# A half-shift of a matrix in memory: half rows cut per queue, or whole rows with wide reads

## The chip, the core and the metric

The kernel runs on one core of a Trainium2 chip. Its time is the device time of one execution in microseconds (us), given as the median of repeated runs. The kernel only moves data: the core has 16 DMA engines which copy from device memory (HBM) to device memory, and two of the core's instruction queues, SP's and ACT's, which hand them the work. No compute engine touches the data.

A word on terms. A DMA instruction names a source pattern and a destination pattern. The hardware turns each into descriptors, each one contiguous run of bytes. A packet, in the profile, is one recorded piece of work of one DMA engine.

## The reference

```
x: 8192 x 8192, float32
out = np.fft.ifftshift(x)
```

For even sizes this swaps the halves along both axes: `out[r, c] = x[(r + 4096) % 8192, (c + 4096) % 8192]`. Each output row is one input row with its left and right half (4096 elements, 16 KB each) exchanged. 268.44 MB are read and as many written. Nothing is computed.

## The kernel before, in words

In the code `R` and `C` are 8192, and `hr` and `hc`, 4096, are half of each. `ENGINES` and `per` are 16, so that one DMA covers `rows` = 256 rows of the output, but of each row only one half: 256 x 16 KB = 4 MB. The helper `copy` (line 29 issues the DMA) takes the queue, the first output row, and `h`, the column at which the written half begins: 0 for the left half, `hc` for the right one. The source half then begins at column `hc - h` of row `(row + hr) % R`.

Both sides of a DMA have the same pattern, in three dimensions: 16 steps of one row, then 16 steps of 16 rows, then 4096 elements side by side. The outermost dimension is the one that is dealt over the 16 DMA engines, so engine e copies rows e, e + 16, e + 32 and so on of the block. At a given moment the 16 engines are thus at work on neighbouring rows, 32 KB apart, and each engine goes on by 512 KB from one descriptor to the next. Every descriptor, read or write, is 16 KB.

The outer loop takes 1024 rows at a time, as four blocks. SP's queue writes the left halves of blocks 0, 1, 2, 3; ACT's queue writes the right halves of blocks 2, 3, 0, 1. The two halves of an output row are therefore written by different queues at different times, and likewise the two halves of an input row are read at different times. Each queue issues 32 DMAs.

The framework gives each DMA a completion semaphore out of four per queue. The first four DMAs of a queue go out at once; each later one waits for the DMA four places ahead of it in the same queue to land. Nothing else orders the work.

Of the kernel before, what the change touches and what calls it, by code (L numbers as in the profile page):

```python
# [1 line left out]

# [4 lines left out]


ENGINES = 16


@with_exitstack
def kernel(
    ctx: ExitStack,
    tc: tile.TileContext,
    x: bass.AP,
    out: bass.AP,
):
    nc = tc.nc
    R, C = x.shape  # L20
    hr = R // 2
    hc = C // 2
    per = 16
    rows = ENGINES * per

    def copy(queue, row, h, step):

        dims = [[C, ENGINES], [step * C, per], [1, hc]]
        queue.dma_start(
            out=bass.AP(out.tensor, out.offset + row * C + h, dims),  # L30
            in_=bass.AP(x.tensor, x.offset + (row + hr) % R * C + hc - h, dims),
        )

    for first in range(0, R, 4 * rows):
        for n in range(4):
            copy(nc.sync, first + n * rows, 0, ENGINES)
            copy(nc.scalar, first + (n + 2) % 4 * rows, hc, ENGINES)


# [1 line left out]
_INS = ['x']  # L43
_OUTS = [((8192, 8192), 'float32')]


def kernel(**inputs):
    import numpy as _np
    import concourse.bacc as _bacc
    import concourse.tile as _tile  # L50
    from concourse import mybir as _mybir
    from concourse.bass_utils import run_bass_kernel_spmd as _run

    nc = _bacc.Bacc("TRN2", target_bir_lowering=False, num_devices=1)  # L54
    arrays, args = {}, []
    for name in _INS:
        a = _np.ascontiguousarray(inputs[name])
        if a.dtype.kind in "iu":
            a = a.astype(_np.int64)
        arrays[f"in_{name}_dram"] = a  # L60
        args.append(nc.dram_tensor(f"in_{name}_dram", a.shape, _mybir.dt.from_np(a.dtype), kind="ExternalInput").ap())
    for i, (shape, dtype) in enumerate(_OUTS):
        dt = _mybir.dt.from_np(_np.dtype(dtype))
        args.append(nc.dram_tensor(f"out_{i}_dram", shape, dt, kind="ExternalOutput").ap())
    with _tile.TileContext(nc) as tc:
        kernel(tc, *args)
    r = _run(nc, [arrays], core_ids=[0])
    got = tuple(r.results[0][f"out_{i}_dram"] for i in range(len(_OUTS)))
    return got[0]
```

## Time and profile before

| what | value |
|---|---|
| time, median of 3 runs (lowest to highest) | 820.25 us (819.56 to 822.04) |
| profiled execution, span from its first to its last instruction | 812.4 us |
| profiled execution, its own device time | not recorded apart; the median lies 7.85 us above the span |
| DMA instructions | 32 on SP's queue, 32 on ACT's, 4 MB each |
| data packets | 16384 of 16 KB, half in each queue |
| mean rate of the copy, one direction | 330 GB/s over the span |
| compute engines | 0.2 us of POOL at the start |

The span begins with four small memory fills that every program of this framework makes. The row of digits for DMA in the page's view by slices is the busy share of the 16 DMA engines in tenths, and the row of GB/s is what they copied, in one direction; memory sees that rate twice, once as reads and once as writes. The view of queues counts the packets, those of a few bytes that raise semaphores among them. The view of DMA issues gives the time from the issue of a DMA to its landing. The view of waits for the DMA queues tells how long a queue stood before it could issue its next DMA, which costs nothing as long as the engines still have work.

### The profile page before, as it was taken

What the parts mean: (1) busy time and instruction counts of PE and PEld (TensorE: products, weight loads), DVE (VectorE), ACT (ScalarE), POOL (GpSimd) and SP (SyncE); (2) the same over time, 40 slices, a digit from 0 to 9 for tenths busy, and PEclk for the clock granted to TensorE, in tenths of its full rate; (3) what the DMA queues carried; (4) which work ended last, traced back from release to release, by engine and by line L of the source; (5) the groups of instructions that cost most, each with busy time, mean ns of one, the idle gap of its engine ahead of it and who ended that gap; (6) DMA issues with size and microseconds to landing.
All of it is one profiled execution on the core that took longest, in us unless ns stands there. A gap on an engine that the chain in (4) does not pass through costs nothing. (4 is left out here: it accounts for less than half of the span.)

```text
span 812.4 us, 109 instructions
## 1 busy us (share of the span) xinstructions
POOL 0.2 (0%) x4
## 2 busy tenths in 40 slices
POOL 0000000000000000000000000000000000000000
DMA  9999999999999999999999999999999999999998
GB/s 307 331 331 336 335 331 331 335 325 337 334 332 336 331 333 332 334 339 332 332 334 331 329 331 334 332 328 333 330 334 335 334 328 333 332 331 330 338 331 280
DMA packets 17408, 268.44 MB, mean 330 GB/s; under 512 B 1024, under 2 KB 1024, under 8 KB 1024
## 3 DMA queue, kind: packets, MB, share of 16 engines
q1 hardware_dynamic: 8704, 134.22, 49.7%
q10 hardware_dynamic: 8704, 134.22, 49.5%
HBM read 268.44 MB, written 268.44 MB: 661 GB/s over the span
## 5 line engine op out<-in xcount | busy, mean ns | idle before, releaser
L54 POOL MEMSET const-bfloat16-1.0<- 128x1 bf16 x1 | 0.1, 101 | 0.0
L54 POOL MEMSET const-uint8-127<- 128x1 uint8 x1 | 0.1, 101 | 0.0
L54 POOL MEMSET const-float32-0.0<- 128x1 f32 x1 | 0.1, 98 | 0.2 <-issue 0.2
L54 POOL MEMSET const-float32-1.0<- 128x1 f32 x1 | 0.1, 98 | 0.0
## 6 DMA issues: line engine op xcount, KB each, us to landing
out_dram<-in_x_dram SPq DMA_DIRECT2D x32, 4096.0 KB, 101.0
out_dram<-in_x_dram ACTq DMA_DIRECT2D x32, 4096.0 KB, 101.0
```

Of the source, the lines that this page charges most:

```text
L54: nc = _bacc.Bacc("TRN2", target_bir_lowering=False, num_devices=1)
```

## The change

Each DMA now takes 256 whole rows (8 MB) instead of 256 half rows (4 MB). The two patterns of a DMA no longer have the same shape. The source is 128 runs of two whole rows, 64 KB each. The destination is 256 rows of two half rows, 16 KB each, the right half first and then, by a negative step, the left one: read in order, the left half of an input row is what the right half of the output row wants. So 64 KB come in by one read descriptor and go out by four write descriptors. Because the ordinary call wants both sides to have the same shape, the DMA instruction is built directly.

The outermost dimension is now 128 long on the source and 256 long on the destination, and each of the 16 engines takes 8 of the one and 16 of the other. For both to mean the same rows, each engine's share must be 16 consecutive rows. At a given moment the 16 engines are thus at work on rows 16 apart, 512 KB, and each engine goes through 512 KB without a jump in the source.

SP's queue takes blocks 0, 2, 4 and so on, ACT's queue blocks 1, 3, 5 and so on. Each issues 16 DMAs, in the same scheme of four semaphores per queue: the first four go out at once and the later ones wait for the one four places ahead.

```
-    per = 16
-    rows = ENGINES * per
+    wide = 2
+    block = 256
-    def copy(queue, row, h, step):
+    def lowered(queue, tensor, offset, dims):
+        return queue.lower_ap_dma(bass.AP(tensor, offset, dims))
-        dims = [[C, ENGINES], [step * C, per], [1, hc]]
-        queue.dma_start(
-            out=bass.AP(out.tensor, out.offset + row * C + h, dims),
-            in_=bass.AP(x.tensor, x.offset + (row + hr) % R * C + hc - h, dims),
+    def copy(queue, name, row):
+        src = x.offset + (row + hr) % R * C
+        dst = out.offset + row * C + hc
+        queue.add_instruction(
+            mybir.InstDMACopy(
+                name=nc.get_next_instruction_name(),
+                queue=name,
+                mode="Copy",
+                ins=lowered(queue, x.tensor, src, [[wide * C, block // wide], [1, 1], [1, wide * C]]),
+                outs=lowered(queue, out.tensor, dst, [[C, block], [-hc, 2], [1, hc]]),
+            )
         )
-    for first in range(0, R, 4 * rows):
-        for n in range(4):
-            copy(nc.sync, first + n * rows, 0, ENGINES)
-            copy(nc.scalar, first + (n + 2) % 4 * rows, hc, ENGINES)
+    for first in range(0, R, 2 * block):
+        copy(nc.sync, "qSPDynamicHW", first)
+        copy(nc.scalar, "qActDynamicHW", first + block)
```

## The prediction

> **What bounds the kernel now.** I read the page's slices first, then its queues and issues, then the waits of the DMA queues, then short windows at both ends. The page by slices, queues and issues:
>
> ```profile
> span 812.4 us, 109 instructions
> ...
> DMA  9999999999999999999999999999999999999998
> GB/s 307 331 331 336 335 331 331 335 325 337 334 332 336 331 333 332 334 339 332 332 334 331 329 331 334 332 328 333 330 334 335 334 328 333 332 331 330 338 331 280
> DMA packets 17408, 268.44 MB, mean 330 GB/s; under 512 B 1024, under 2 KB 1024, under 8 KB 1024
> ...
> q1 hardware_dynamic: 8704, 134.22, 49.7%
> q10 hardware_dynamic: 8704, 134.22, 49.5%
> HBM read 268.44 MB, written 268.44 MB: 661 GB/s over the span
> ...
> out_dram<-in_x_dram SPq DMA_DIRECT2D x32, 4096.0 KB, 101.0
> out_dram<-in_x_dram ACTq DMA_DIRECT2D x32, 4096.0 KB, 101.0
> ```
>
> The engines hold packets for 99.2% of the span (49.7 + 49.5), so no idle time between DMAs is left to win. The rate is flat: apart from the first and the last slice of 20.3 us it lies between 325 and 339 GB/s. The 17408 packets are 16384 of data and 1024 of a few bytes for semaphores. One data packet takes on average 0.992 x 812.4 us x 16 / 16384 = 787 ns. Among the packet records of this trace the shortest full packets, and a quarter of all of them, take about 611 ns; many take over 1000. An engine can thus pass 16 KB in 611 ns, or 429 GB/s over 16 engines, and mostly does not: on average 176 ns of a packet, 22%, are waiting within it. Since neither queue nor engine is idle, I put this waiting down to memory, which serves 661 GB/s of reads and writes together. Which part of memory it is, this trace doesn't show.
>
> The waits of the DMA queues, with their total, number and longest in us:
>
> ```profile
> SPq L29 <- DMA out_dram<-in_x_dram: 689.4, 28, 25.3
> SPq L65 <- DMA out_dram<-in_x_dram: 102.2, 2, 79.5
> ```
>
> SP's queue waits 28 times, about 25 us each, but a DMA lands 101 us after its issue. Four are always under way, so these waits starve no engine. Short windows at both ends (start and end, us, POOL, clock, DMA share, GB/s):
>
> ```profile
> 0.00:2.00 2.00, 0.20 (x4) 1.00 0.00 0
> 2.00:4.00 2.00, 0.00 (x0) 1.00 1.03 336
> ...
> 806.00:808.00 2.00, 0.00 (x0) 1.00 0.96 328
> 808.00:810.00 2.00, 0.00 (x0) 1.00 0.54 180
> 810.00:812.40 2.40, 0.00 (x0) 1.00 0.02 7
> ```
>
> The data moves from 2.0 us to about 809.5, that is 807.5 us at 332.4 GB/s, with some 5 us of edges. The sum is made against this execution: span 812.4, and the median of the runs, 820.25, is 7.85 more; I carry these 7.85 over unchanged.
>
> **The change part by part.**
>
> *Fewer descriptors.* Reads go from 16384 to 4096; writes stay at 16384. What a descriptor costs by itself is bounded by the small packets: the 4-byte semaphore packets take 9 ns, and an 8 KB record of 307 ns against the 611 leaves 611 - 2 x 307, below zero, so nothing. An engine handles 768 read descriptors fewer (12288 / 16): 0 to 768 x 9 ns = 6.9 us. I take 0, since a cost of 9 ns lies under the 176 ns that the mean packet waits for memory anyway; if memory stopped being the limit, up to 6.9 us would come free.
>
> *Half as many DMAs.* 32 instead of 64, so per engine 32 semaphore packets fewer: 32 x 9 ns = 0.3 us off. The issue itself (571 ns on SP's queue, 578 on ACT's) happens beside running transfers, except the first, which keeps its place: data still starts at about 2.0 us. There are 12 waits for a DMA four ahead on each queue instead of 28. With 8 MB per DMA each queue gets half of 332.4 GB/s and lands one in about 50 us, some 200 us after issue. Behind each wait stands only the next DMA of the same queue, with three more under way: 0.
>
> *The end.* All engines carry 16.8 MB as before, and now end in the records within about 2.4 us of each other. If an engine turns from one queue to the other only after a 64 KB read, that unit takes 4 x 787 ns = 3.1 us instead of 0.8, and the last engine can be late by up to the difference. Bounds 0 and +2.4 us; I take +1, between them, because the present spread is already about three small units.
>
> *The order in which memory is touched.* This is the term that decides. Before, each engine reads and writes 16 KB and jumps 512 KB; the two halves of a row are used at different times. After, each engine runs through 512 KB of source in order, and the destination in order but for the swap within each 32 KB row. On the other hand the engines stand 512 KB apart instead of 32 KB, in step at the start of every DMA. No row of the trace prices either. The bounds: at best the wait within packets disappears, 1024 packets x 611 ns = 626 us of transfer instead of 807.5, -181 us. At worst the rate is that of the poorest short slice; the DMA view of the last 112 us, in slices of 2.8 us, shows them:
>
> ```profile
> GB/s 304 357 363 281 357 328 351 345 310 334 316 328 334 357 298 351 304 369 316 293 427 281 363 310 351 304 363 363 298 339 310 357 334 322 304 351 357 304 310 29
> ```
>
> Apart from the end the poorest is 281: 268.44 MB / 281 GB/s = 955 us, +148. Both ends are extremes of a moment that the average never held. The rows nearest to a steady pattern are the 20 us slices: 339 GB/s at best and 325 at worst, i.e. 792 us (-15.6) or 826 us (+18.5). [...]
>
> As a limit on the gain, the Trainium skill (HBM Reference, Specifications) gives a memory domain about 716 GB/s. The trace's 661 agrees in being below it; 536.9 MB at 716 would be an estimated 750 us of transfer, and the sum with it about 763 us, so by that page a large part of the 181 us is out of reach.
>
> **The sum.** 820.25 - 15.6 (order) + 1.0 (end) - 0.3 (semaphores) + 0 (descriptors, waits) = 805.4 us. I say 805.
>
> **The rivals.**
>
> *Streams collide (slower).* The sixteen engines stand at a distance of a power of two, 512 KB, twice (for reads and for writes). If they ask the same part of memory at once, the waiting within packets grows. Place: the 176 ns per packet. Price: at the poorest 20 us slice, 325 GB/s, 820.25 + 18.5 + 0.7 = 839; half way from there to the poorest short slice, 303 GB/s, 886 us transfer and 899. It decides as soon as the mean packet is over 787 ns, whatever the reads gain. For it: packet times scatter from 611 to over 1000 ns, so memory already reacts to which addresses meet; the old order kept the engines on neighbouring rows. Against it: the scatter soon takes engines out of step, within one DMA of 32 units each. Chance 0.37.
>
> The Trainium skill speaks for this rival (DMA: Bandwidth & Descriptors, Latency and other measured facts): copies with rows a large power of two apart lose rate, 207 GB/s at a pitch of 512 KiB against 214 in full, and 164 at 2 MiB. Taken over to the distance between engines, that ratio is an estimated 807.5 x 214/207 = 835 us of transfer and 848 us in all; no run here shows it yet.
>
> *Nothing moves.* Memory serves 661 GB/s whatever the order, and only the end and the semaphores differ: 820.25 + 1 - 0.3 = 821. For it: the flat slices, 325 to 339 all along, while SP and ACT meet different addresses. Against it: nobody has shown that the 22% of waiting is indifferent to order. Chance 0.09.
>
> *Only the descriptors pay.* The read side has a fixed cost which is on the path after all: 820.25 - 3.5 (half of the 6.9) + 0.7 = 817. Chance 0.07.
>
> *The read is taken whole before it is written,* or the wide read is not spread over 16 engines. If a 64 KB read and its four writes no longer overlapped, a 64 KB unit would take up to twice 4 x 611 ns; 256 units x 4.9 us = 1251 us. Against it: 128 and 256 both divide by 16, and in the present trace reads and writes share one packet of 611 ns. Chance 0.06.
>
> *The change doesn't do what it says.* The hardware may cut the 64 KB reads into 16 KB. Then the order in memory still changes, and the forecast or the first rival holds; only the 3.1 us unit falls away. No chance of its own.
>
> **How the numbers follow.** The forecast's case, a better rate, has 0.41; its own range is 789 to 817, from twice the step of the best slice down to a quarter of it. A measurement of this kernel tells 0.3%, or 2.5 us, from no change, which is the band 817.8 to 822.7. Faster: 0.41 + 0.07 = 0.48. Same: 0.09. Slower: 0.37 + 0.06 = 0.43. The range must take in much of the slower cases: from 782 (two and a half such steps; 0.04 below) to 880, which leaves out the 0.06 of unoverlapped reads and about 0.09 of heavy collisions.
>
> **What would show it.** DMA packets: 4096 of 64 KB if the wide read is the unit, 16384 if the writes are. DMA share still about 99%, mean rate 339, issues x16 with 8192 KB landing in about 200 us. A collision shows as the same share with under 330 GB/s; a lost overlap as a rate under 250; uneven engines as a long last slice. What would make me wrong is above all the one term of memory order, chosen between +148 and -181 by the nearest slices.

## The result and the profile after

The changed kernel takes 867.58 us (median of 4 runs, 867.10 to 868.31) against 821.10 us for the kernel before measured beside it (median of 4, 819.56 to 822.04): a ratio of 1.0567, 95% interval 1.0544 to 1.0590. It is slower by 5.7%. The forecast was 805, so the sign is wrong, though the range reached to 880. Of the times and ratios below, one leaves a run out: the kernel with shares of 15 rows took 832.29 to 836.07 us in three runs and 868.30 in a fourth, which is not counted.

The page of the changed kernel, with the lines that answer to those shown before:

```profile
span 865.4 us, 77 instructions
...
DMA  9999999999999999999999999999999999999998
GB/s 285 311 310 311 309 314 314 314 312 305 307 315 313 313 304 311 310 314 317 305 317 313 314 314 311 310 315 314 312 314 304 313 314 316 307 310 314 316 309 276
DMA packets 16896, 268.44 MB, mean 310 GB/s; under 512 B 512, under 2 KB 512, under 8 KB 512
...
q10 hardware_dynamic: 8448, 134.22, 49.9%
q1 hardware_dynamic: 8448, 134.22, 49.5%
HBM read 268.44 MB, written 268.44 MB: 620 GB/s over the span
...
out_dram<-in_x_dram ACTq DMA_DIRECT2D x16, 8192.0 KB, 215.0
out_dram<-in_x_dram SPq DMA_DIRECT2D x16, 8192.0 KB, 215.2
```

Three things are to be seen. First, the loss is spread evenly: the engines hold packets for 99.4% of the span, as before, but the rate is 304 to 317 GB/s in the inner slices instead of 325 to 339. A data packet takes 0.994 x 865.4 us x 16 / 16384 = 840 ns on average instead of 787; 16384 / 16 = 1024 packets per engine times those 53 ns are 54 us, and the span grew by 53.0. Nothing is lost between packets or at the ends. Second, of the 16896 packets 512 raise semaphores and 16384 carry data, 16 KB each. There is no packet of 64 KB. Third, a DMA lands 215 us after its issue, where some 200 were foreseen.

The 53.0 us between the spans are more than the 46.5 by which the times differ, because the two profiles do not match: in every run that has both, the time is 1.7 to 2.2 us above the span, so the profiled execution of the kernel before took an estimated 814 us, less than any of its four timed runs. The 7.85 us that the prediction carried over were mostly this difference between executions.

The short windows of the changed kernel (start and end, us, POOL, clock, DMA share, GB/s) show the same start and a short end:

```profile
2.00:4.00 2.00, 0.00 (x0) 1.00 0.98 262
...
200.00:400.00 200.00, 0.00 (x0) 1.00 1.00 311
400.00:600.00 200.00, 0.00 (x0) 1.00 1.00 313
...
860.00:862.00 2.00, 0.00 (x0) 1.00 1.00 295
862.00:865.40 3.40, 0.00 (x0) 1.00 0.33 106
```

The source line of the issue has one surprise, in ns, as least, median and greatest; the kernel before comes first:

```profile
L29 SPq DMA_DIRECT2D out_dram<-in_x_dram x32: 571/571/652, 0.7 to 708.6; - x32
...
L36 SPq DMA_DIRECT2D out_dram<-in_x_dram x16: 554/43836/50956, 0.7 to 647.1; - x16
```

An issue took 0.57 us before and now typically 43.8: the queue is held for that long before it can go on. That looks like a cause, and the experiments test it.

What the compiler made of the change can be read from the DMA instruction itself, as pairs of step (in elements) and count:

```
before         source  [8192, 16] [131072, 16] [1, 4096]
               dest    [8192, 16] [131072, 16] [1, 4096]
changed kernel source  [4096, 512] [1, 1] [1, 4096]
               dest    [8192, 256] [-4096, 2] [1, 4096]
```

The source asked for 128 runs of two rows. Lowering it against a destination with pieces of 4096 elements cut it into 512 pieces of 16 KB, one behind the other. So the wide reads of 64 KB, of which the change was to be made, are not in the instruction; the encoded length of a source piece is 16384 bytes. What is left of the change is the order of addresses, the larger DMA, and a source and a destination whose patterns are no longer alike: one dimension of 512 here, 256 by 2 there. Two descriptions of equal length and equal piece, but of unlike shape.

### The profile page after: what moved, and what is told of

The parts are those of the page before. It is cut to its first block, busy times and chain, and to the rows that moved or that the text cites. A ratio compares the mean times of both kernels' runs of the same rounds, so it can differ in the third digit from the quotient of the medians.

```text
span 865.4 us, 77 instructions
## 1 busy us (share of the span) xinstructions
POOL 0.2 (0%) x4
## 2 busy tenths in 40 slices
DMA packets 16896, 268.44 MB, mean 310 GB/s; under 512 B 512, under 2 KB 512, under 8 KB 512
```

## The experiments

All times are medians; every ratio is to the kernel before measured beside it, with its 95% interval. There the kernel before took 812 to 814 us.

**First: which part of the change costs it?** Theory 1 was the distance of 512 KB between the engines, the rival of the prediction.

Engines 512 KB apart, half rows as before:

```
-        dims = [[C, ENGINES], [step * C, per], [1, hc]]
+        dims = [[step * C, ENGINES], [C, per], [1, hc]]
```

> The kernel before with one edit: engine e takes rows 16e to 16e+15 of the block instead of e, e+16, e+32. The engines are then 512 KB apart, as in the changed kernel; half rows, 4 MB DMAs and the pairing of the queues stay. Theory 1 (the distance of 512 KB between the engines costs the time): 855 to 875 us, rate near 310 GB/s. Rival A (the reads, DMA size or the two halves in one DMA cost it): 815 to 826 us.

Measured: 812.26 us, 1.0004 (0.9978 to 1.0030). The distance alone costs nothing.

The source written as 16 KB reads:

```
-ins=lowered(..., src, [[wide * C, block // wide], [1, 1], [1, wide * C]])
+ins=lowered(..., src, [[C, block], [hc, 2], [1, hc]])
```

> The changed kernel with the source pattern written as two half rows of 16 KB per row, in the same order of addresses. Since the compiled instruction of the changed kernel already holds 512 reads of 16 KB, all theories that I still hold expect 865 to 870 us. The theory that wide reads cost the time expects 815 to 830 us.

Measured: 848.39 us, 1.0449 (1.0412 to 1.0485). It compiles to the same DMA instructions as the changed kernel, so this is also a second measurement of that: 4.5% here, 5.7% in the first comparison, where the kernel before was slower too (821.1 against 812.3). Its span of 846.9 us gives 822 ns for a data packet, so 35 of the 53 ns above come back, and 36 of the 46.5 us. Why the same instructions cost more in the first comparison is not explained.

Shares of 15 rows instead of 16:

```
-    block = 256
+    share = 15      # blocks of 240 rows; the last 16 rows of each half as one small DMA
```

> The changed kernel in blocks of 240 rows (a rest of 16 rows in each half of the matrix goes as one small DMA): engines are 15 rows, 480 KB, apart instead of 16 rows, 512 KB. Theory 1a (what costs is that the distance is a power of two): 800 to 830 us. Theory 1b (what costs is that engines are far apart at all): 860 to 875 us. Rival A (DMA size or the halves in one DMA): 860 to 875 us.

Measured: 834.15 us, 1.0289 (1.0234 to 1.0344), between the two expectations. With theory 1 gone this told little by itself; it finds its place below.

DMAs of 8 MB, rows dealt as before:

```
-    per = 16
+    per = 32
-            copy(nc.scalar, first + (n + 2) % 4 * rows, hc, ENGINES)
+            copy(nc.scalar, first + (n ^ 1) * rows, hc, ENGINES)
```

> The kernel before with 512 rows in a DMA instead of 256, that is 8 MB as in the changed kernel, with the queues still 16 MB apart; rows are dealt to the engines as before. Theory 1: 817 to 824 us, though the queues now block in the issue for some 44 us per DMA. Rival B (DMAs too large for the queue, whose issue blocks): 850 to 875 us.

Measured: 813.45 us, 1.0009 (0.9977 to 1.0041), with an issue of 41.1 us at the median on SP's queue. So the long issue by itself costs nothing.

**Second: the queues' distance, or neighbouring halves?** Theory 2 blamed the 8 MB between the queues; theory 3 the step from one half of a row straight to the other.

```
 queues 8 MB apart (kernel before):
-            copy(nc.scalar, first + (n + 2) % 4 * rows, hc, ENGINES)
+            copy(nc.scalar, first + (n ^ 1) * rows, hc, ENGINES)
```

> The kernel before with the queues 256 rows (8 MB) apart instead of 512 rows (16 MB); nothing else. Theory 2 (the two queues at 8 MB, not 16 MB, collide): about 4.5 per cent over the kernel before, 845 to 860 us. Theory 3 (what costs is that one queue of an engine takes both halves of a row one right after the other): within 0.5 per cent of before.

Measured: 812.15 us, 0.9995 (0.9970 to 1.0020).

```
 queues 16 MB apart (changed kernel):
-        copy(nc.scalar, "qActDynamicHW", first + block)
+        for row in (first, first + block):      # first in steps of 4 * block
+            copy(nc.sync, "qSPDynamicHW", row)
+            copy(nc.scalar, "qActDynamicHW", row + 2 * block)
```

> The changed kernel with the queues 512 rows (16 MB) apart instead of 256 rows. Theory 2: within 1 per cent of the kernel before. Theory 3: 4 to 6 per cent over it, as the changed kernel.

Measured: 850.16 us, 1.0454 (1.0418 to 1.0491). Theory 2 falls with these two.

```
 the other half first (changed kernel):
-        ins ... [[wide * C, block // wide], [1, 1], [1, wide * C]]   outs ... [[C, block], [-hc, 2], [1, hc]]
+        ins ... [[C, block], [-hc, 2], [1, hc]]                      outs ... [[C, block], [hc, 2], [1, hc]]
```

> The changed kernel with the two halves of each row taken in the other order: the source goes right half, left half, and the destination is written in order. Theory 3, and theory 2 too: 4 to 6 per cent over the kernel before. If only the backward step of the writes were at fault, within 1 per cent of the kernel before.

Measured: 848.05 us, 1.0413 (1.0398 to 1.0429). Writing backwards is not the fault. Note that now the destination is the single run of 512 pieces and the source is 256 by 2.

```
 halves in two DMAs (kernel before, shares of 16 rows):
+        for h in (hc, 0):
+            copy(nc.sync, first, h, ENGINES)
+            copy(nc.scalar, first + rows, h, ENGINES)
```

> Whole rows in the changed kernel's order of blocks and with its engine shares (16 consecutive rows) and queues 8 MB apart, but each block as two half-row DMAs of 4 MB one behind the other, first the right halves, then the left ones. Theory 2: 4 to 6 per cent over the kernel before. Theory 3: within 1 per cent of it, since a queue now meets the second half of a row only 16 descriptors per engine later.

Measured: 813.08 us, 0.9985 (0.9969 to 1.0002). Theory 3 stood here, four expectations out of four.

**Third: what about the neighbouring halves?**

```
 left half of one block, right half of the next, by turns:
-        ins ... [[wide * C, block // wide], [1, 1], [1, wide * C]]   outs ... [[C, block], [-hc, 2], [1, hc]]
+        ins ... [[C, block], [other * C + hc, 2], [1, hc]]           outs ... [[C, block], [other * C - hc, 2], [1, hc]]
```

> Still half rows of 16 KB, 8 MB DMAs and shares of 16 rows, and still left and right halves by turns in one DMA as in the changed kernel, but the right half belongs to the row 256 rows further on (on ACT's queue, further back). No two descriptors in a row touch neighbouring memory any more. Theory 3 (the cost is that an engine's queue goes from one half of a row straight to the other, 16 KB away): within 1 per cent of the kernel before. Rival C (the pattern of a DMA with two halves by turns costs it, wherever they lie): 4 to 6 per cent over it.

Measured: 815.17 us, 1.0012 (0.9990 to 1.0034), as theory 3 expects; but this run is not clean, since the framework took the writes of the two queues for overlapping and let ACT's DMAs wait for SP's. It shows by accident what the long issue hangs on. The two queues issue DMAs of the same size, but ACT's has only one or two under way, as one lands after 61.7 us and the next goes out about 50 us after the last:

```profile
L35 SPq DMA_DIRECT2D out_dram<-in_x_dram x16: 573/40488/48138, 0.7 to 582.5; - x16
L35 ACTq DMA_DIRECT2D out_dram<-in_x_dram x16: 580/582/648, 28.5 to 784.9; - x16
```

In the changed kernel, too, the first three issues of each queue take under 1 us, and the fourth is the first to be held. The hold goes with what already waits in the queue, not with the size of one DMA alone.

```
 no exchange of columns, right half before left on both sides:
-        ins ... [[wide * C, block // wide], [1, 1], [1, wide * C]]
+        ins ... [[C, block], [-hc, 2], [1, hc]]      # src begins at + hc
```

> The changed kernel without the exchange of left and right (the columns stay, so that part of the computation is left out): both sides go right half, left half, row by row. Neighbouring halves follow each other, but neither side is one unbroken run that hardware could join to longer pieces. Theory 3a (neighbouring halves in a row cost it by themselves): 4 to 6 per cent over the kernel before. Theory 3b (it costs only where one side is an unbroken run and the other not): within 1 per cent.

Measured: 813.30 us, 0.9995 (0.9976 to 1.0013). Neighbouring halves are free: theory 3 falls as first put, and 3b or something about the exchange is left.

```
 one row per engine and DMA:
-    block = 256
+    block = 16
```

> The changed kernel in blocks of 16 rows, so that an engine takes one row of a DMA (two descriptors) and the engines are one row, 32 KB, apart as in the kernel before; 512 DMAs of 512 KB. Theory 3 alone: 4 to 6 per cent over the kernel before. If the neighbouring halves cost only together with a great distance of the engines (as the 2.9 per cent at 15 rows suggests): within 1 per cent of it. Issue: 256 DMAs per queue, each about 0.6 us, against 3.2 us that a queue has for one, so nothing from there.

Measured: 819.29 us, 1.0068 (1.0048 to 1.0088), within the second expectation.

```
 64 KB on both sides, no exchange:
-        outs ... [[C, block], [-hc, 2], [1, hc]]
+        outs ... [[wide * C, block // wide], [1, 1], [1, wide * C]]
```

> Whole rows without the exchange of left and right (that part of the computation is left out), with 64 KB descriptors on both sides, engines 512 KB apart, 8 MB DMAs: what wide descriptors are worth where both sides can have them. Theory 3a: 4 to 6 per cent over the kernel before, since an engine runs through neighbouring memory. My prediction's view (long runs help memory): 1 to 4 per cent under it.

Measured: 813.82 us, 0.9995 (0.9978 to 1.0011). Its page shows that wide descriptors would have been visible as packets:

```profile
DMA packets 4608, 268.44 MB, mean 331 GB/s; under 512 B 512, under 2 KB 512, under 8 KB 512
...
HBM read 268.44 MB, written 268.44 MB: 661 GB/s over the span
```

4608 less 512 for semaphores are 4096 packets of 64 KB. They run at the rate of the kernel before, neither better nor worse: the view that long runs help memory is refuted here, where long runs really exist.

**Fourth: do reads and writes meet in memory?** Theory 4 held that an engine reads one half while it writes the same half 4096 rows away.

```
 kernel before, both queues on the same rows:
-            copy(nc.scalar, first + (n + 2) % 4 * rows, hc, ENGINES)
+            copy(nc.scalar, first + n * rows, hc, ENGINES)
```

> The kernel before with ACT's queue on the same rows as SP's instead of 512 rows away, so that an engine alternates between the two halves of the same rows, one queue reading the half that the other is writing the counterpart of. Theory 4 (reads and writes collide when one engine reads column half h of an input row while it writes column half h of the output row exactly 4096 rows from it, so at an unchanging distance of 128 MB in the two tensors): 2 to 6 per cent over the kernel before. Rival D (the cost needs both halves as consecutive descriptors of one DMA): within 0.7 per cent.

Measured: 813.30 us, 0.9990 (0.9963 to 1.0017).

```
 changed kernel, source 256 rows further on:
-        src = x.offset + (row + hr) % R * C
+        src = x.offset + (row + hr + block) % R * C
```

> The changed kernel with the source 256 rows (8 MB) further on, so that the rows are shifted by 4352 instead of 4096 (that part of the computation is altered); order, halves and shares stay. Theory 4: within 1 per cent of the kernel before, since the halves read and written together no longer stand exactly 128 MB apart. Rival D (neighbouring halves taken in exchange cost it, wherever the rows are written to): 4 to 6 per cent over it.

Measured: 847.99 us, 1.0431 (1.0399 to 1.0464). Against theory 4 on both counts.

```
 changed kernel, four rows per engine and DMA:
-    block = 256
+    block = 64
```

> The changed kernel in blocks of 64 rows: the engines are 4 rows, 128 KB, apart, queues 2 MB apart, 2 MB a DMA. With 32 KB between the engines the loss was 0.7 per cent, with 512 KB 4 to 5.7. If the loss grows with the distance of the engines: 1 to 4 per cent over the kernel before. If it needs the great distance: under 1 per cent.

Measured: 811.84 us, 0.9980 (0.9958 to 1.0003). This was the strangest so far: the changed kernel's order, halves and exchange, in 2 MB pieces, at the speed of the kernel before.

```
 as the queues on the same rows, with shares of 16 rows:
+        dims = [[step * C, ENGINES], [C, per], [1, hc]]
+            copy(nc.scalar, first + n * rows, hc, ENGINES)
```

> The kernel before with both edits at once: ACT's queue on the same rows as SP's, and shares of 16 consecutive rows, so that the engines are 512 KB apart. Theory 4, with the distance making it worse: 4 to 6 per cent over the kernel before and more than with the rows dealt out. Rival D: within 0.7 per cent.

Measured: 813.53 us, 1.0003 (0.9981 to 1.0025). Theory 4 is dead.

**Fifth: order of addresses, or unlike patterns?** All slow kernels up to here have the unlike patterns described above, and every DMA in them that matters is large. Two kernels take the pair apart. The trick is to begin the second half of a source row 256 bytes early: the two halves then no longer join to one run, and the source keeps its shape of 256 by 2.

```
 like patterns, the changed kernel's order with the exchange:
-        ins ... [[wide * C, block // wide], [1, 1], [1, wide * C]]
+        ins ... [[C, block], [hc - 64, 2], [1, hc]]
 compiled: source [8192, 256] [4032, 2] [1, 4096]   dest [8192, 256] [-4096, 2] [1, 4096]
```

> The changed kernel, but the second half of each source row begins 64 elements (256 bytes) earlier, so that source and destination keep the same shape of 256 rows by 2 halves, where the compiled source of the changed kernel is one run of 512 pieces of 16 KB. The addresses are otherwise the same (64 columns of each left half come out altered). Theory 5 (the order of addresses costs it: neighbouring halves, exchanged, with engines 512 KB apart): 4 to 6 per cent over the kernel before. Theory 6 (the unlike patterns of the two sides cost it, in DMAs of some size): within 1 per cent of the kernel before.

```
 unlike patterns, a plain copy without the exchange:
+        ins ... [[C, block], [hc - 64, 2], [1, hc]]
+        outs ... [[C, block], [hc, 2], [1, hc]]       # dst begins at row * C
 compiled: source [8192, 256] [4032, 2] [1, 4096]   dest [4096, 512] [1, 1] [1, 4096]
```

> Whole rows without the exchange of left and right (left out; 64 columns of each right half come out altered too), with the source in 256 rows by 2 halves, the second 256 bytes early, and the destination as one run of 512 pieces of 16 KB. Theory 5: within 1 per cent of the kernel before, like the kernels without the exchange. Theory 6: 3 to 6 per cent over it, with the addresses of a plain copy.

Measured: like patterns 813.61 us, 1.0016 (0.9996 to 1.0037); unlike patterns 847.01 us, 1.0438 (1.0390 to 1.0485). The pages, like patterns first:

```profile
span 810.8 us, 77 instructions
...
DMA packets 16896, 268.44 MB, mean 331 GB/s; under 512 B 512, under 2 KB 512, under 8 KB 512
...
HBM read 268.44 MB, written 268.44 MB: 662 GB/s over the span
```

and the unlike ones:

```profile
span 844.1 us, 77 instructions
...
DMA packets 16896, 268.44 MB, mean 318 GB/s; under 512 B 512, under 2 KB 512, under 8 KB 512
...
HBM read 268.44 MB, written 268.44 MB: 636 GB/s over the span
```

The same packets, the same number of DMAs of the same size, the same early 256 bytes. The changed kernel's addresses without its unlike patterns are as fast as the kernel before; a plain copy with unlike patterns is as slow as the changed kernel. Theory 6 holds so far: it is the description of the two sides, not where the data lies.

One thing is not taken apart. In every slow kernel one side is a single dimension of 512 pieces (480 with shares of 15 rows) and the other side is not. No run has 512 pieces of 16 KB in one dimension on both sides, or two unlike sides of which neither is such a run. That the unlikeness costs the time, and not the one long dimension by itself, is therefore argued, not shown; 64 KB on both sides has one dimension on each and is fast, but with 8 pieces per engine it is also small in pieces.

A view of the issues of the like kernel, in ns, closes the other suspicion:

```profile
L35 SPq DMA_DIRECT2D out_dram<-in_x_dram x16: 573/41074/46916, 0.7 to 607.0; - x16
```

It is held for 41 us per issue just as the slow one is for 44, and loses nothing by it.

The size belongs to it. With unlike patterns, by pieces of 16 KB that one engine gets from one DMA:

| pieces per engine and DMA | rows in a block | ratio to the kernel before |
|---|---|---|
| 2 | 16 | 1.0068 |
| 8 | 64 | 0.9980 |
| 30 | 240 | 1.0289 |
| 32 | 256 | 1.0413 to 1.0567 |

The 0.7% of the first line may be its 512 DMAs; no run separates that. Where between 8 and 30 the loss begins was not tried.

The large ones are also those whose issue is held: in the kernel with 64 rows SP's median issue is 553 ns. It would fit that the loss comes from handing out the descriptors, or from a full queue. The end of the traces speaks against both, as far as they would have to act while the data moves. In the kernel with unlike patterns the last issue is over at 677.5 us, and from 793.5 us on only the last DMA of each queue is under way; in the one with like patterns this is so from 650.6 and 762.8 us on. The rates before and after the second moment, unlike patterns first:

```profile
680.00:790.00 110.00, 0.00 (x0) 1.00 1.00 319
794.00:838.00 44.00, 0.00 (x0) 1.00 0.99 320
```

```profile
652.00:760.00 108.00, 0.00 (x0) 1.00 1.00 332
764.00:805.00 41.00, 0.00 (x0) 1.00 0.99 334
```

The loss of 4% stays when nothing is being issued, and when an engine has at most 32 pieces left from each queue. The kernel with 64 rows has as many under way, four DMAs of 8 pieces, and loses nothing. So, as far as these traces reach, the loss goes with the size of the single DMA and not with how much is under way. What happens inside such a DMA stays open: no trace here separates a packet's wait for its descriptor from its wait for memory.

## Why the prediction was wrong

The sum failed at two terms. The order of addresses was put at -15.6 us and is worth nothing. And the sum had no term for what the change did to the patterns of a DMA, which is the whole loss: with the order at 0 it gives 821 us, and the 46.6 us from there to 867.6 are missing, or 34 to 36 by the later comparisons. That 867.6 still lies in the stated range is luck, since the range went up to 880 for collisions, which no run shows.

*The change doesn't do what it says.* This was the rival to which I gave no chance of its own, and it is what happened: the reads were cut to 16 KB, as the 16384 data packets and the compiled pattern show, though by the lowering and not by the hardware. I wrote that then only the order in memory remains. That was the blind spot: the two patterns had also become unlike, one of them a single long dimension, and this is where the time went. The patterns after lowering could have been read before the run; I read only the source text.

*The order in which memory is touched,* taken at -15.6 us, is the step of the sum that failed. No run shows a gain from it. With like patterns the changed kernel's order measures +0.16% (-0.04 to +0.37), or about +1 us, and real 64 KB runs -0.05% (-0.22 to +0.11). The right value was 0. Picking the best 20 us slice as a price was not a bound on anything: the slices of one kernel scatter by themselves, and say nothing of another pattern.

*Streams collide* came close in its time (839, or 899 for the heavier case, against 867.6) and lay on the right side, but not by its mechanism: engines 512 KB apart cost 1.0004. The rule that I set beside it, the Trainium skill (DMA: Bandwidth & Descriptors, Latency and other measured facts), has rows 512 KiB apart at 207 GB/s against 214. Carried over to the distance between engines it would have given some 3%; the runs measure 0.0% (-0.2 to +0.3), so it doesn't carry over to this pattern. That the estimate from it, 848 us, is what the same instructions took in the later comparisons (847 to 850) is chance.

*Fewer descriptors* at 0: right, though the reads did not become fewer. Where they truly do, with 64 KB on both sides, nothing is gained either, so the 0 to 6.9 us that was kept as a bound is closed at its lower end.

*Half as many DMAs,* waits at 0: right. The 8 MB DMAs alone measure 1.0009. The landing was put at 200 us; it is 202 with like patterns and 215 in the changed kernel. But I had the issue at 0.57 us, and it is 44. It stayed hidden, as the 8 MB DMAs alone show; I take it that this is because several DMAs are always under way.

*The end,* +1 us: there is no 64 KB unit, so its reason is gone. The last window holds 106 GB/s over 3.4 us, 0.36 MB, or 1.2 us at the usual rate.

*The limit on the rate.* The waiting within packets that I put down to memory is 176 ns in the kernel before. Of what the change added to a packet, 53 ns in the first comparison and 35 in the second, none that the runs can tell is due to the order of addresses in memory, as the like and unlike kernels show. Whether the 176 ns are, is still open: the kernels with like patterns all stand at 658 to 665 GB/s whatever their order, which fits a common ceiling and does not name it.

## What to carry to other kernels

When a DMA is written with a different pattern on each side, read what the compiler made of both before reasoning about descriptor sizes: a contiguous side may be folded into one long dimension and cut to the piece size of the other. Keep the two sides alike in their dimensions in large DMAs, or keep the DMAs small; here the same rows in 64-row blocks, or nearly the same addresses with like patterns, cost nothing. And when the packets get longer while engines stay full, memory is only one suspect: change the description of a transfer without its addresses, and its addresses without the description.

## What was not expected of the hardware

- Copies in the same order, but for 256 bytes, differ by 4% with the shape of their patterns: 813.6 us with 256 by 2 on both sides, 847 to 850 in the later comparisons with 512 on one of them.
- The order of addresses is worth nothing over a wide field. Engines 32 KB or 512 KB apart, queues on the same rows or 8 or 16 MB apart, halves together or apart, 16 or 64 KB pieces: with like patterns all lie between 0.9985 and 1.0016.
- With up to four DMAs of 32 pieces per engine under way in a queue, an issue holds it for 41 to 44 us at the median; with 8 pieces of 64 KB for the same 8 MB, 0.5 us, and with one or two DMAs of 32 pieces under way, 0.58. It costs no time here, but a queue that has other work would stand still for it.
